# Up products of a half block in two groups by weight part, and w2's pieces loaded in queue order, on one Trainium2 core

## The chip, the cores and the metric

The kernel runs on one core of one Trainium2 chip. The metric is the device time of one execution in microseconds, the median of several runs; lower is better. Before the change it is 1317.91 us (three runs, 1317.73 to 1318.84).

## What is computed

A trunk of two layers over 256 tokens of 1,024 features. Each layer has a feed-forward stage, a mixer and a second feed-forward stage, each followed by a layer norm:

```python
def swiglu(x, w1, w3, w2):
    return (jax.nn.silu(x @ w1) * (x @ w3)) @ w2

for l in range(DEPTH):                       # DEPTH = 2
    x = layer_norm(ALPHA * x + 0.5 * swiglu(x, ffn_w1[l, 0], ffn_w3[l, 0], ffn_w2[l, 0]), ...)
    y, v_raw = hybrid_mixer(x, w_in[l], ..., w_out[l], ...)
    x = layer_norm(ALPHA * x + y, ...)
    x = layer_norm(ALPHA * x + 0.5 * swiglu(x, ffn_w1[l, 1], ffn_w3[l, 1], ffn_w2[l, 1]), ...)
```

w1 and w3 are 1,024 x 2,816, w2 is 2,816 x 1,024, all float32. The mixer (a recurrent branch, a gated branch and a linear recurrence, merged by gates) isn't touched by the change.

## The kernel before

Every large product is made of float32 values split in two: a high part, rounded to the type that TensorE multiplies in one pass, and a low part, the rest. A weight tile is loaded by SP's queue into a raw buffer (`_load`, L73), cast to its high part on ScalarE (L94), and its low part is the difference of the two, on VectorE (L96). The class `Weights` holds all weight tiles of the program in one list in the order of use. It loads some tiles ahead of the conversion and converts four tiles ahead of the use. Tiles of w1 and w3 (four contraction blocks of 128 rows by 256 columns, 512 KB) go through a shared pool of three raw buffers and a ring of five converted pairs. Pieces of w2 (128 rows by 1,024 columns, 512 KB) go through raw buffers of their own, three too, and six converted pairs, both held by the feed-forward stage.

A feed-forward stage takes the 2,816 inner features in 11 blocks of 256. The first block is computed with tokens on the partitions (rows `w1t`, `w3t`). For the other ten, `up(j)` computes features by tokens: for w1 and then for w3, two half blocks of 128 features, each into one PSUM bank (rows `w`). A half block is `feature_wide`: for each of the eight contraction blocks one product of the weights' high part with both parts of the activations, 512 columns (L318), and one of the weights' low part with the activations' high part, 256 columns (L319). The high part's two results lie side by side in the bank, and VectorE adds them (L391). Then comes the gate, and its split into `g`. From the third block on, each `up` is followed by the down products of a block two earlier (rows `dn`, lines L204 to L206 in `mm3`, all 512 columns): 24 products in a row. The last three blocks' down products stand at the end of the stage.

So a stage has ten blocks of four half blocks of 16 products; the four stages of the program have 160 half blocks, 1,280 products of each of the two kinds.

The order in which instructions stand on each engine is made by a planner that knows dependencies, priorities and its own estimate of durations; it moves an instruction ahead of others of its engine when it takes it to be ready. `issue_after` forbids it to put what is issued inside ahead of a given instruction. A load waits for its raw buffer, and SP's queue takes its loads in order.

Of the kernel before, what the change touches and what calls it, by code (L numbers as in the profile page):

```python
# [12 lines left out]
P = 128  # L13
# [39 lines left out]
class Weights:  # L53


    def __init__(self, tc, raw, part, ahead, load_ahead):
        self.nc, self.tc = tc.nc, tc
        self.raw, self.part = raw, part
        self.ahead, self.load_ahead = ahead, load_ahead
        self.queue, self.raws, self.parts = [], {}, {}  # L60
        self.own_raw = None
        self.nload = self.nconv = self.nused = self.hp = 0

    def add(self, key, ap, own=False, pool=False):
# [3 lines left out]
    def _load(self):  # L68
        i = self.nload
        ap = self.queue[i][1]  # L70
        raw = self.own_raw if self.queue[i][2] and self.own_raw else self.raw
        t = raw.tile([P, ap.shape[1], ap.shape[2]], F32, tag="raw", name=f"raw{i}", bufs=3)
        self.last_load = self.nc.sync.dma_start(t, ap).ins  # L73
        self.raws[i] = t
        self.nload += 1

# [42 lines left out]
class Trunk:  # L119
# [193 lines left out]
    def feature_wide(self, out, ws, m):  # L313

        mm = self.nc.tensor.matmul
        for k in range(8):
            hi, lo = (t[:, k % 4, m * P:(m + 1) * P] for t in ws[k // 4])
            mm(out, hi, self.xT2[:, :, k, :], start=k == 0, stop=False)  # L318
            mm(out[:, 0, :], lo, self.xT[0][:, k, :], start=False, stop=k == 7)  # L319

    def queue_block(self, key, w, c0, pool=False):
        for q in range(2):
# [219 lines left out]
class Mixer:  # L542
# [63 lines left out]
    def mm(self, shape, what):  # L606
        return self.T.bank(self.T.mm, shape, what)
# [836 lines left out]
```

## Time and profile before

| what | before |
|---|---|
| median of the runs | 1317.91 us |
| profiled execution | 1319.23 us |
| its span | 1317.5 us |
| TensorE busy | 1289.8 us, 98% of the span |
| VectorE busy | 940.1 us, 71% |
| ScalarE busy | 656.3 us, 50% |
| DMA, mean over the span | 174 GB/s |

The span is the time from the first to the last instruction of the profiled execution; the rest of its 1319.23 us lies around it. An engine is busy while at least one of its instructions is recorded as running. TensorE's products overlap, and the ends in the record are modelled, so the distance between the starts of two products tells what one costs. In the span the feed-forward stages lie at about 8 to 195, 470 to 655, 655 to 842 and 1125 to 1317 us, the mixers between the first and second, and between the third and fourth.

### The profile page before, as it was taken

Reading aid. Unit: us, or ns where it says so; the run is one execution under the profiler, and the core shown is the slowest. Engines: PE = TensorE matmul, PEld = TensorE weight load, DVE = VectorE, ACT = ScalarE, POOL = GpSimd, SP = SyncE. Lnnn points to the kernel's source line nnn. Section 1 sums busy time; section 2 is a strip of 40 time slices with the busy share of each in tenths; the row PEclk is TensorE's granted clock in tenths of the full one; section 3 lists DMA queues with packets and bytes.
Section 4 is the critical chain, followed back from the end, with each engine's and each line's share of the span. In section 5 each row is a group of like instructions: output and inputs, shape, how many; then the busy total and the mean of one; then the engine's idle time right before and its main releaser. Section 6 shows DMA issues by size and latency. Waiting matters only on the chain.

```text
span 1317.5 us, 23323 instructions
## 1 busy us (share of the span) xinstructions
PE 1289.8 (98%) x9527; PEld 1157.5 (88%) x9527; DVE 940.1 (71%) x1311; ACT 656.3 (50%) x881; POOL 84.1 (6%) x147
## 2 busy tenths in 40 slices
PE   9999999998999999999999999999989999999997
PEld 8888889997899988888898888999978998888886
DVE  7786666787676687766686766667867567876664
ACT  6454425655845555444264544275557444544440
POOL 1000000003000110000000000001030002100000
PEclk9999999999999999999999999999989999999999
DMA  9886534534246668665379664264432466776630
GB/s 334 243 265 190 176 96 129 174 114 130 83 129 193 208 228 283 192 189 169 91 271 293 200 187 138 67 185 129 129 98 82 144 210 207 258 246 188 189 111 32
DMA packets 184540, 229.83 MB, mean 174 GB/s; under 512 B 8145, under 2 KB 165841, under 8 KB 184433
## 3 DMA queue, kind: packets, MB, share of 16 engines
q1 hardware_dynamic: 183792, 226.24, 55.5%
q0 software_dynamic: 640, 2.10, 0.5%
q8 instruction: 75, 1.23, 0.4%
q14 instruction: 33, 0.26, 0.1%
HBM read 227.26 MB, written 1.05 MB: 173 GB/s over the span
## 4 chain that ended last, share of the span: by engine, by line
PE 89%; DVE 4%; ACT 3%; POOL 2%; issue 2%; DMA 0%; SPq 0%; DVEq 0%; ACTq 0%; POOLq 0%
PE w L318 23%; PE w L319 11%; PE dn L204 6%; PE dn L205 6%; PE dn L206 6%; PE gate L205 3%; PE gate L204 3%; PE gate L206 3%; PE zr L206 2%; PE zr L205 2%; PE zr L204 2%; PE pb L205 2%; PE pb L206 2%; PE pb L204 2%; DVE wlo L96 1%
## 5 line engine op out<-in xcount | busy, mean ns | idle before, releaser
L94 ACT CAST whi<-raw 128x1024 fp32r<-128x1024 f32 (+1 forms) x322 | 331.7, 1035 | 353.3 <-issue 80.4
L96 DVE TENSOR_TENSOR wlo<-raw,whi 128x1024 fp32r<-128x1024 f32 (+1 forms) x314 | 378.3, 1209 | 166.9 <-ACT whi L94 163.1
L318 PE MATMUL w<-xT,whi 128*128 128x512 f32 x1280 | 452.5, 398 | 0.0
L319 PE MATMUL w<-xT,wlo 128*128 128x256 f32 x1280 | 356.6, 281 | 0.1
L318 PEld LDWEIGHTS w<-xT,whi 128*128 128x128 f32 x1280 | 239.5, 188 | 57.4
L319 PEld LDWEIGHTS w<-xT,wlo 128*128 128x128 f32 x1280 | 241.6, 189 | 3.3 <-DVE wlo L96 0.5
L205 PE MATMUL dn<-w,g 128*128 128x512 f32 x352 | 137.4, 390 | 0.0
L204 PE MATMUL dn<-w,g 128*128 128x512 f32 x352 | 137.1, 391 | 0.0
L206 PE MATMUL dn<-w,g 128*128 128x512 f32 x352 | 137.0, 390 | 0.0
L96 DVE TENSOR_TENSOR w<-raw,w 128x1024 fp32r<-128x1024 f32 x88 | 104.9, 1226 | 37.4 <-ACT w L94 37.4
L391 DVE TENSOR_REDUCE h<-w 128x256 f32<-128x512 f32 x160 | 109.6, 686 | 15.9 <-PE w L319 14.3
L204 PE MATMUL gate<-xT,whi 128*128 128x256 f32 x384 | 110.1, 287 | 1.3 <-DVE xc L1158 1.3
L205 PE MATMUL gate<-xT,whi 128*128 128x256 f32 x384 | 109.7, 286 | 0.0
L206 PE MATMUL gate<-xT,wlo 128*128 128x256 f32 x384 | 109.6, 285 | 0.0
L94 ACT CAST w<-raw 128x1024 fp32r<-128x1024 f32 x88 | 88.7, 1048 | 32.6 <-PE dn L206 23.1
L204 PEld LDWEIGHTS dn<-w,g 128*128 128x128 f32 x352 | 66.1, 188 | 14.6 <-ACT g L209 0.2
L206 PEld LDWEIGHTS dn<-w,g 128*128 128x128 f32 x352 | 66.1, 188 | 14.1
L205 PEld LDWEIGHTS dn<-w,g 128*128 128x128 f32 x352 | 66.1, 188 | 12.2
L204 PEld LDWEIGHTS gate<-xT,whi 128*128 128x128 f32 x384 | 73.4, 191 | 2.5 <-issue 2.2
L205 PEld LDWEIGHTS gate<-xT,whi 128*128 128x128 f32 x384 | 73.4, 191 | 0.8 <-issue 0.2
L206 PEld LDWEIGHTS gate<-xT,wlo 128*128 128x128 f32 x384 | 73.4, 191 | 0.6 <-issue 0.2
L206 PE MATMUL zr<-xT,wlo 128*128 128x256 f32 x224 | 63.9, 285 | 0.0
(333 smaller groups left out, 2205.4 us busy)
## 6 DMA issues: line engine op xcount, KB each, us to landing
raw<-in_ffn_w_dram SPq DMA_DIRECT2D x264, 512.0 KB, 4.6
raw<-in_w_in_dram SPq DMA_DIRECT2D x108, 512.0 KB, 4.1
raw<-in_p_branch_dram SPq DMA_DIRECT2D x24, 512.0 KB, 3.4
raw<-in_w_out_dram SPq DMA_DIRECT2D x16, 512.0 KB, 4.1
ln_g<-in_ln_g_dram SPq DMA_DIRECT2D x8, 256.0 KB, 6.9
ln_b<-in_ln_b_dram SPq DMA_DIRECT2D x8, 256.0 KB, 7.3
bd<-in_bd_dram SPq DMA_DIRECT2D x6, 256.0 KB, 6.0
ln_g<-in_ln_g_dram POOLq DMA_DIRECT2D x4, 256.0 KB, 4.1
```

The costliest lines, as they stand in the source:

```text
L94: self.last_act = self.nc.scalar.copy(hi[:, s:s + w], t[:, s:s + w]).ins
L96: eng.tensor_tensor(lo[:, s:s + w], t[:, s:s + w], hi[:, s:s + w], ALU.subtract)
L204: mm(out, a[0], b[0], start=start, stop=False)
L205: mm(out, a[0], b[1], start=False, stop=False)
L206: mm(out, a[1], b[0], start=False, stop=stop)
L318: mm(out, hi, self.xT2[:, :, k, :], start=k == 0, stop=False)
L319: mm(out[:, 0, :], lo, self.xT[0][:, k, :], start=False, stop=k == 7)
L391: nc.vector.tensor_reduce(t[:, m, :], b.rearrange("p a s -> p s a"), mybir.AxisListType.X, ALU.add)
```

## The change

It has two parts. In `feature_wide` the sixteen products of a half block are written as two loops, the eight of the high part first, then the eight of the low part. A list of the sixteen weight slices is made ahead of them, and the first product still clears the bank and the last closes it. In `_load` a load into a w2 raw buffer may not stand ahead of the last load into a shared raw buffer that was written before it.

```diff
--- before.py
+++ after.py
@@ -58,7 +58,7 @@
         self.raw, self.part = raw, part
         self.ahead, self.load_ahead = ahead, load_ahead
         self.queue, self.raws, self.parts = [], {}, {}
-        self.own_raw = None
+        self.own_raw = self.last_shared = None
         self.nload = self.nconv = self.nused = self.hp = 0
 
     def add(self, key, ap, own=False, pool=False):
@@ -70,7 +70,13 @@
         ap = self.queue[i][1]
         raw = self.own_raw if self.queue[i][2] and self.own_raw else self.raw
         t = raw.tile([P, ap.shape[1], ap.shape[2]], F32, tag="raw", name=f"raw{i}", bufs=3)
-        self.last_load = self.nc.sync.dma_start(t, ap).ins
+        with ExitStack() as order:
+
+            if raw is not self.raw and self.last_shared is not None:
+                order.enter_context(self.tc.issue_after(self.last_shared))
+            self.last_load = self.nc.sync.dma_start(t, ap).ins
+        if raw is self.raw:
+            self.last_shared = self.last_load
         self.raws[i] = t
         self.nload += 1
 
@@ -313,10 +319,11 @@
     def feature_wide(self, out, ws, m):
 
         mm = self.nc.tensor.matmul
+        parts = [[t[:, k % 4, m * P:(m + 1) * P] for k in range(8) for t in ws[k // 4][i:i + 1]] for i in range(2)]
         for k in range(8):
-            hi, lo = (t[:, k % 4, m * P:(m + 1) * P] for t in ws[k // 4])
-            mm(out, hi, self.xT2[:, :, k, :], start=k == 0, stop=False)
-            mm(out[:, 0, :], lo, self.xT[0][:, k, :], start=False, stop=k == 7)
+            mm(out, parts[0][k], self.xT2[:, :, k, :], start=k == 0, stop=False)
+        for k in range(8):
+            mm(out[:, 0, :], parts[1][k], self.xT[0][:, k, :], start=False, stop=k == 7)
 
     def queue_block(self, key, w, c0, pool=False):
         for q in range(2):
```

What this does to the instructions is seen on two engines. TensorE, first stage, right behind the first run of down products: `w_57_656` is the PSUM bank of a half block, `xT_104` the activations, `whi_548` and `whi_554` the high parts of its two weight tiles, `wlo_549` and `wlo_555` the low parts. Before:

```order
L206 MATMUL dn_616<-w_36_505,g_19_378 128x512
L318 MATMUL w_57_656<-xT_104,whi_548 128x512
L319 MATMUL w_57_656<-xT_104,wlo_549 128x256
L318 MATMUL w_57_656<-xT_104,whi_548 128x512
L319 MATMUL w_57_656<-xT_104,wlo_549 128x256
L318 MATMUL w_57_656<-xT_104,whi_548 128x512
L319 MATMUL w_57_656<-xT_104,wlo_549 128x256
L318 MATMUL w_57_656<-xT_104,whi_548 128x512
L319 MATMUL w_57_656<-xT_104,wlo_549 128x256
L318 MATMUL w_57_656<-xT_104,whi_554 128x512
L319 MATMUL w_57_656<-xT_104,wlo_555 128x256
L318 MATMUL w_57_656<-xT_104,whi_554 128x512
```

and now, where a row with x4 is four instructions that read alike:

```order
L212 MATMUL dn_616<-w_36_505,g_19_378 128x512
L324 MATMUL w_57_656<-xT_104,whi_548 128x512 x4
L324 MATMUL w_57_656<-xT_104,whi_554 128x512 x4
L326 MATMUL w_57_656<-xT_104,wlo_549 128x256 x4
L326 MATMUL w_57_656<-xT_104,wlo_555 128x256 x4
L324 MATMUL w_58_674<-xT_104,whi_548 128x512 x4
L324 MATMUL w_58_674<-xT_104,whi_554 128x512 x4
L326 MATMUL w_58_674<-xT_104,wlo_549 128x256 x4
L326 MATMUL w_58_674<-xT_104,wlo_555 128x256 x4
```

The wide products (512) and the narrow ones (256) alternated and now stand in runs of eight; the second half block (`w_58_674`) follows in the same way. Over the whole program there are 160 runs of eight wide and 160 of eight narrow products.

SP's queue at the program's start, behind the loads of the activations and of the first three tiles: tiles of 128x4x256 are w1 and w3, those of 128x1024 are pieces of w2. Before:

```order
L1361 DMA x_94<-in_x_dram 128x1024
L73 DMA raw_381<-in_ffn_w_dram 128x1024
L73 DMA raw_387<-in_ffn_w_dram 128x1024
L73 DMA raw_546<-in_ffn_w_dram 128x1024
L73 DMA raw_142<-in_ffn_w_dram 128x4x256
L73 DMA raw_159<-in_ffn_w_dram 128x4x256
L73 DMA raw_165<-in_ffn_w_dram 128x4x256
L73 DMA raw_552<-in_ffn_w_dram 128x1024
L73 DMA raw_692<-in_ffn_w_dram 128x1024
L73 DMA raw_698<-in_ffn_w_dram 128x1024
L73 DMA raw_227<-in_ffn_w_dram 128x4x256
L73 DMA raw_229<-in_ffn_w_dram 128x4x256
```

and now:

```order
L1368 DMA x_94<-in_x_dram 128x1024
L77 DMA raw_142<-in_ffn_w_dram 128x4x256
L77 DMA raw_159<-in_ffn_w_dram 128x4x256
L77 DMA raw_165<-in_ffn_w_dram 128x4x256
L77 DMA raw_227<-in_ffn_w_dram 128x4x256
L77 DMA raw_229<-in_ffn_w_dram 128x4x256
L77 DMA raw_231<-in_ffn_w_dram 128x4x256
L77 DMA raw_237<-in_ffn_w_dram 128x4x256
L77 DMA raw_243<-in_ffn_w_dram 128x4x256
L77 DMA raw_249<-in_ffn_w_dram 128x4x256
L77 DMA raw_381<-in_ffn_w_dram 128x1024
L77 DMA raw_387<-in_ffn_w_dram 128x1024
```

The pieces of w2 (`raw_381`, `raw_387`, `raw_546` and so on) stood among the first tiles and now follow the tiles that are used ahead of them; their conversions on ScalarE and VectorE moved in the same way. In the later stages the pieces of w2 are put in turn likewise.

## Rows read from the trace of the kernel before

**Rows 1.** The page: TensorE's busy time (share, instructions), granted clock in 40 slices.

```profile
PE 1289.8 (98%) x9527; PEld 1157.5 (88%) x9527; DVE 940.1 (71%) x1311; ACT 656.3 (50%) x881; POOL 84.1 (6%) x147
PEclk9999999999999999999999999999989999999999
```

**Rows 2.** Stretches: us; length; busy us by engine (instructions); clock; DMA share; GB/s.

```profile
330.00:394.00 64.00, 61.37 (x964) 58.13 (x963) 44.47 (x81) 42.84 (x66) 3.26 (x2) 1.00 0.37 109
...
490.00:655.00 165.00, 165.00 (x867) 140.69 (x866) 113.22 (x133) 72.13 (x83) 0.92 (x1) 1.00 0.63 194
...
1140.00:1300.00 160.00, 160.00 (x846) 136.66 (x845) 105.62 (x120) 68.96 (x78) 0.00 (x0) 1.00 0.57 181
```

**Rows 3.** The page's groups: line, engine, names, shapes, count, busy us, mean ns, idle.

```profile
L318 PE MATMUL w<-xT,whi 128*128 128x512 f32 x1280 | 452.5, 398 | 0.0
L319 PE MATMUL w<-xT,wlo 128*128 128x256 f32 x1280 | 356.6, 281 | 0.1
...
L204 PEld LDWEIGHTS gate<-xT,whi 128*128 128x128 f32 x384 | 73.4, 191 | 2.5 <-issue 2.2
```

**Rows 4.** Timeline of TensorE: start us, length us, instruction; down run, up block, down run.

```profile
62.48 0.39 PE L204 MATMUL dn<-w,g 128*128 128x512 f32 x1
...
67.95 0.39 PE L318 MATMUL w<-xT,whi 128*128 128x512 f32 x1
...
79.26 0.39 PE L204 MATMUL dn<-w,g 128*128 128x512 f32 x1
```

**Rows 5.** The same timeline, start of the second feed-forward stage, 17 pairs apart.

```profile
485.11 0.40 PE L318 MATMUL w<-xT,whi 128*128 128x512 f32 x1
...
491.00 0.39 PE L318 MATMUL w<-xT,whi 128*128 128x512 f32 x1
```

**Rows 6.** The same timeline, gate products of layer 0's mixer, 102 products apart.

```profile
406.16 0.28 PE L204 MATMUL gate<-xT,whi 128*128 128x256 f32 x1
...
418.40 0.28 PE L204 MATMUL gate<-xT,whi 128*128 128x256 f32 x1
```

**Rows 7.** Timeline: ninth down product after 62.48; first and 84th of the output projection.

```profile
64.32 0.39 PE L206 MATMUL dn<-w,g 128*128 128x512 f32 x1
...
445.90 0.39 PE L204 MATMUL wo<-whi,mg 128*128 128x512 f32 x1
...
465.12 0.39 PE L206 MATMUL wo<-whi,mg 128*128 128x512 f32 x1
```

**Rows 8.** Timeline: places where up products of one kind already are neighbours.

```profile
31.88 0.88 PE L318 MATMUL w<-xT,whi 128*128 128x512 f32 x3
32.59 0.28 PE L319 MATMUL w<-xT,wlo 128*128 128x256 f32 x1
...
483.00 0.40 PE L318 MATMUL w<-xT,whi 128*128 128x512 f32 x1
...
483.70 0.64 PE L318 MATMUL w<-xT,whi 128*128 128x512 f32 x2
...
484.87 0.40 PE L319 MATMUL w<-xT,wlo 128*128 128x256 f32 x2
```

**Rows 9.** Timeline of VectorE and TensorE at the start, with idle time before and its releaser.

```profile
16.17 2.35 DVE L96 TENSOR_TENSOR w<-raw,w 128x1024 fp32r<-128x1024 f32 x2
18.43 1.22 DVE L96 TENSOR_TENSOR wlo<-raw,whi 128x1024 fp32r<-128x1024 f32 x1
...
18.85 0.40 PE L204 MATMUL w3t<-whi,xT 128*128 128x256 f32 x2
19.71 0.39 PE L205 MATMUL w3t<-wlo,xT 128*128 128x256 f32 x1 [0.46 <-DVE wlo L96]
...
28.42 0.71 PE L318 MATMUL w<-xT,whi 128*128 128x512 f32 x2
...
29.41 0.39 PE L318 MATMUL w<-xT,whi 128*128 128x512 f32 x1
```

**Rows 10.** The page's DMA issues: what, queue, count, KB each, median us to landing.

```profile
raw<-in_ffn_w_dram SPq DMA_DIRECT2D x264, 512.0 KB, 4.6
```

## Prediction

> **What bounds the kernel now.** I began with the page's busy times and its clock line [rows 1]: TensorE holds work in 98% of the span, and its granted clock is at the upper level, 2.4 GHz, in nearly all forty slices. The table of stretches comes next, because the change touches the four feed-forward stages alone [rows 2]: in the two stretches of feed-forward that stand there TensorE has no idle time at all, while the mixer's stretch shown (layer 0, 330 to 394 us) idles 2.6 us. So inside the stages that change, time can only come from how fast TensorE takes its instructions, or from the few waits at the program's start. A busy TensorE is no TensorE at its peak, since a product's recorded length (398 ns for a wide one, 281 for a narrow one, [rows 3]) overlaps the next; I go by distances between starts.
>
> **What an up product costs now.** Between two runs of down products lie 32 pairs, one wide product of the high part (512 columns) and one narrow product of the low part (256). From the first wide start at 67.95 to the first down start at 79.26 is 11.31 us [rows 4], 353.4 ns a pair. There are 1,280 pairs [rows 3], so about 452 us. The pace has a second value: from 485.11 to 491.00 stand 17 pairs, 346.5 ns each [rows 5]. Such stretches cover about 100 pairs, all near the start of stages two to four; 1,180 run at the slower pace. The same two shapes, each among its own kind, give the quicker sum: 102 narrow gate products take 12.24 us, 120.0 ns each [rows 6], and the last 16 of a run of 24 down products, all 512 wide, go from 64.32 to 67.95, 226.9 ns each [rows 4, 7]; 120.0 + 226.9 = 346.9. So alternating costs some 6.5 ns a pair in most places, and a run of one kind seems not to pay it.
>
> **The change part by part.** First, the sequence. No instruction is added or removed: eight wide, then eight narrow products for each of 160 half blocks, 16 instructions each. The printed order shows no half block mixed with another any more; before, a handful near the stages' starts were. Price of eight narrow: 8 x 120.0 = 960 ns [rows 6]; other rows put two neighbours at 118 each (484.87 to 485.11) [rows 5, 8], so 117 to 120 are the ends and I take 120, since the gate products have the same operands. Price of eight wide is the open term, as before never has more than three in a row. Nearest below: 226.9, a settled down run. Nearest above: the three wide ones at 31.88, which reach to 32.59, 237 each [rows 8]. Between them lies the start of a down run, entered from a narrow product as each run of eight will be: its first eight go from 62.48 to 64.32, 230.0 each [rows 4, 7]; and the output projection's 512-wide products never settle, 83 of them at 231.6 [rows 7]. I take 230.0: eight are too few to settle. A half block then takes 8 x 230.0 + 960 = 2,800 ns against 8 x 353.4 = 2,827. For the 1,180 pairs (147.5 half blocks) that is 147.5 x 27 = 4.0 us less; the 12.5 half blocks at 8 x 346.5 = 2,772 lose 12.5 x 28 = 0.35 us. Net -3.6 us. That one pair of equal neighbours already helps is seen at 483.00: six wide and six narrow with one such meeting of each kind take 2.11 us to 485.11, where six pairs at 353.4 take 2.12 [rows 5, 8].
>
> The row on a weight load speaks against a run of narrow products: a load is recorded with 191 ns for a gate product [rows 3]. Were that exclusive, eight narrow would take 1,528 ns and the kernel some 87 us more; but the gates start every 120 ns with a load each [rows 6], so the record overlaps and the load isn't the limit. The Trainium skill ("TensorE: Matmul & The Clock Gate", section "LDWEIGHTS (loading the stationary operand)") gives the columns over 1.2 GHz, an estimate of 107 ns for 128 columns; by that a load fits under a narrow product, with little to spare, and a run of eight costs no more than the gates' 120.
>
> Second, the waits on weights. With the high part first, the low part's subtraction on DVE is needed 8 x 230 = 1.8 us later in a half block; the second tile's high part is needed after 4 x 0.23 = 0.9 us, not after 4 x 0.353 = 1.4. The first tile's low part is held 2.3 us into the second half instead of 1.4, so its buffer comes back 0.9 us later, with a ring of five tiles and two more halves, 5.6 us, before the next block. As no TensorE wait stands in those stretches [rows 2], I cost this at nothing; without that cover it would be at most 0.9 us a block.
>
> Third, w2's pieces asked for in turn. On SP's queue three pieces of w2, needed only by the first down run, stood ahead of the fourth tile of w1/w3, and more after it; now the first pieces stand behind twelve tiles. Their conversions went ahead as well: DVE works on two w2 pieces from 16.17 and only at 18.43 on the low part that TensorE then waits for [rows 9]. Two waits follow: at 18.85 two narrow products take 0.86 us instead of 0.24; at 28.42 two wide and a narrow one take 0.99 instead of 0.57 [rows 9]. Both should go: -1.0 us. Nothing else is late there: the load in question moves up by three places of 512 KB. Later in each stage w2 is queued behind the other loads and its conversions stand in turn on ACT and DVE. SP's queue now stands behind a piece that waits for a free buffer, and the w1/w3 loads with it; but three raw and five converted buffers let them run eight tiles ahead, at four tiles in 16.8 us [rows 4] over 30 us, against 4.6 us to land [rows 10]. Costed at nothing. The planner also shifted some instructions of layer 0's mixer around 320 to 400 us; the stretch idles 2.6 us [rows 2], so I allow 1.5 us either way.
>
> Sum: -3.6 - 1.0 = -4.6 us. The profiled execution took 1319.23 us around a span of 1317.5; the median of the runs is 1317.9. The sum holds against either, and against the median it gives 1313.3.
>
> **The rivals.** (a) Runs of eight settle at once: 8 x 226.9 + 960 = 2,775 ns, 52 less for 147.5 half blocks, -7.7, with the start's -1.0: 1309.2. For it: the good stretch has exactly this pace although the kinds alternate there [rows 5]. Against it: down runs need about five products to get there [rows 7]. (b) The neighbour doesn't matter: a product costs what its width gives, and only the start improves: 1316.9. For it: two narrow in a row at 118, three wide at 237, sum 355, no better than a pair now [rows 8]. The Trainium skill's section "Back-to-back issue gap" on the same page is such a rule, N/2.4 + 2.5 ns, estimates of 216 and 109 ns that the order can't alter; the rows above are 11 ns longer each and show two paces for one mix, so I give it less than the forecast. (c) Slower: the wide product reads two planes of the activations, and a run of such reads on TensorE costs 237 each, as at 31.88: 8 x 237 + 960 = 2,856, 29 more for 147.5 half blocks and 84 more for 12.5, +5.3, less 1.0: 1322.2. It decides from a mean of 233 ns in the run of eight, (2,827 - 960) / 8. Against it: those three fell on a spot just restarted after a wait. (d) w2 in turn comes too late for the down products: each of 36 runs of down products would have to wait, 0.2 us would be enough for +7 less 4.6: 1320.5. The lead of 30 us speaks against it. That the order isn't what the change says is excluded by the printed order.
>
> **How the numbers follow.** Forecast 0.43, (a) 0.23, (b) 0.22, (c) 0.08, (d) 0.04. A change of 0.2%, 2.6 us, is about what a measurement of this kernel can tell from none. Forecast and (a) are faster, 0.66; (b) is within, 0.22; (c) and (d) slower, 0.12. The forecast's own range, with 1.5 us for the mixer, is 1311.8 to 1314.8; the range reaches to (a) and (b), 1308.7 to 1317.6.
>
> **What would show it.** In the trace after, from the first wide start after a down run to the next down start: 11.20 us by the forecast (4 half blocks), 11.10 by (a), 11.31 by (b), 11.42 by (c). Inside a half block the first wide products should stand 230 or more apart and the last near 227. The first up product should start near 21.8 us instead of 22.45, with no wait at 18.9 and 28.4. A new idle time of TensorE in a feed-forward stretch, ended by ACT, DVE or a DMA, would prove the costs at nothing wrong.

## The result: 1.0093 times the time before

The changed kernel takes 1331.08 us (median of four runs, 1329.24 to 1333.86) beside 1317.82 us for the kernel before (four runs, 1317.68 to 1318.84): a ratio of 1.0093, 95% interval 1.0081 to 1.0105, 13.3 us slower. The prediction said 1313.3 us, at most 1317.6. The profiled execution after has a span of 1332.2 us, 14.7 more than the one before.

The page after, to be held against [rows 1] and [rows 3]: TensorE's busy time and clock, the chain that ended last by engine, and the groups of the up products and of ScalarE's casts of w2 (whose tiles are called w; the casts of w1 and w3 write whi):

```profile
PE 1295.6 (97%) x9527; PEld 1163.9 (87%) x9527; DVE 935.0 (70%) x1311; ACT 649.5 (49%) x881; POOL 83.4 (6%) x147
PEclk9999999989999999999999999999989999999999
PE 72%; DVE 9%; DMA 8%; ACT 4%; issue 4%; POOL 2%; SPq 0%; DVEq 0%; ACTq 0%; POOLq 0%
L324 PE MATMUL w<-xT,whi 128*128 128x512 f32 x1280 | 321.4, 393 | 5.7 <-DVE h L398 5.6
L100 ACT CAST w<-raw 128x1024 fp32r<-128x1024 f32 x88 | 92.0, 1050 | 172.1 <-DMA raw<-in_ffn_w_dram 172.1
```

and from the page before, the chain and the casts of w2:

```profile
PE 89%; DVE 4%; ACT 3%; POOL 2%; issue 2%; DMA 0%; SPq 0%; DVEq 0%; ACTq 0%; POOLq 0%
L94 ACT CAST w<-raw 128x1024 fp32r<-128x1024 f32 x88 | 88.7, 1048 | 32.6 <-PE dn L206 23.1
```

TensorE waits 5.6 us for VectorE's reductions (h) ahead of wide up products, where [rows 3] has 0.0. ScalarE waited 172.1 us for w2 to land; before, it idled 32.6 us ahead of these casts, most of it for TensorE. DMA has 8% of the chain that ended last; it was 0% before. One more slice of the clock line shows an 8.

The stretch of [rows 2] from 490 to 655 us, in two pieces (the same columns):

```profile
490.00:630.00 140.00, 140.00 (x754) 121.10 (x753) 88.02 (x101) 59.26 (x67) 0.00 (x0) 1.00 0.64 209
630.00:655.00 25.00, 22.65 (x113) 18.55 (x112) 22.44 (x26) 16.18 (x19) 0.00 (x0) 1.00 0.65 208
```

So the stretch still has no idle time over most of its length, and 2.35 us of it in its last 25 us, towards the stage's end. That is where this stage loses. By the starts of the first and the last down product of each stage, after minus before:

| stretch | before, us | after, us | difference |
|---|---|---|---|
| start to a down run at one place, [rows 4] 62.48 | 62.48 | 60.52 | -2.0 |
| rest of the first feed-forward | 134.5 | 138.0 | +3.5 |
| first mixer | 308.1 | 313.5 | +5.3 |
| second feed-forward | 151.2 | 153.5 | +2.3 |
| between second and third | 35.4 | 35.4 | 0.0 |
| third feed-forward | 151.2 | 154.0 | +2.7 |
| second mixer | 316.1 | 317.8 | +1.8 |
| fourth feed-forward | 150.4 | 151.4 | +1.1 |

They add up to 14.7 us.

**The up block in the middle of a stage** did what the prediction wanted. TensorE's timeline after (start, length, instruction, count), the answer to [rows 4]:

```profile
148.88 0.40 PE L212 MATMUL dn<-w,g 128*128 128x512 f32 x1
149.11 2.00 PE L324 MATMUL w<-xT,whi 128*128 128x512 f32 x8
150.95 1.11 PE L326 MATMUL w<-xT,wlo 128*128 128x256 f32 x8
151.90 2.00 PE L324 MATMUL w<-xT,whi 128*128 128x512 f32 x8
...
160.28 0.39 PE L210 MATMUL dn<-w,g 128*128 128x512 f32 x1
```

Eight wide take 1.84 us (230.0 each), eight narrow 0.95 us (119 each), the block 149.11 to 160.28, 11.17 us against 11.31. From one down run to the next it is 16.63 us, 16.78 before. Inside a run of eight the wide products stand 233, 236, 228, 233 and 231 ns apart and then 227 (medians over the program's runs): as the prediction said, the first ones 230 or more, the last near 227.

**The last two blocks** are another matter. The same timeline right behind, now with idle time before a row and what ended it:

```profile
165.50 0.39 PE L212 MATMUL dn<-w,g 128*128 128x512 f32 x1
166.64 2.08 PE L324 MATMUL w<-xT,whi 128*128 128x512 f32 x8 [0.75 <-DVE h L398]
...
171.36 1.11 PE L326 MATMUL w<-xT,wlo 128*128 128x256 f32 x8
173.52 2.08 PE L324 MATMUL w<-xT,whi 128*128 128x512 f32 x8 [1.05 <-DVE h L398]
...
179.18 0.39 PE L210 MATMUL dn<-w,g 128*128 128x512 f32 x1
...
185.85 0.50 PE L210 MATMUL dn<-w,g 128*128 128x512 f32 x1 [1.06 <-ACT g L215]
```

This cycle takes 18.90 us. From the start of the last down run to its last six products it is 18.08 us, where 15.78 stood before. Who is late shows in the timelines of ScalarE and VectorE over the same time:

```profile
157.31 0.62 ACT L215 CAST g<-gf 128x512 fp32r<-128x512 f32 x1 [1.89 <-DVE gf L381]
163.59 1.05 ACT L100 CAST w<-raw 128x1024 fp32r<-128x1024 f32 x1 [5.66 <-DMA raw<-in_ffn_w_dram]
164.86 1.05 ACT L100 CAST w<-raw 128x1024 fp32r<-128x1024 f32 x1 [0.23 <-DMA raw<-in_ffn_w_dram]
165.82 1.99 ACT L100 CAST whi<-raw 128x1024 fp32r<-128x1024 f32 x2
167.71 1.05 ACT L100 CAST w<-raw 128x1024 fp32r<-128x1024 f32 x1
169.32 1.05 ACT L100 CAST w<-raw 128x1024 fp32r<-128x1024 f32 x1 [0.56 <-DMA raw<-in_ffn_w_dram]
170.28 0.62 ACT L380 ACTIVATE sl<-h 128x512 f32<-128x512 f32 x1
```

```profile
157.96 0.69 DVE L216 TENSOR_TENSOR g<-gf,g 128x512 fp32r<-128x512 f32 x1 [0.69 <-ACT g L215]
164.67 1.23 DVE L102 TENSOR_TENSOR w<-raw,w 128x1024 fp32r<-128x1024 f32 x1 [6.01 <-ACT w L100]
165.81 0.68 DVE L398 TENSOR_REDUCE h<-w 128x256 f32<-128x512 f32 x1
```

Read it backwards. TensorE's wide products at 166.64 need a PSUM bank, which the reduction of 165.81 empties. That reduction stands behind w2's low part on VectorE, which waited 6.01 us for ScalarE's cast, which waited 5.66 us for a piece of w2 to land. Its load and two more were issued behind one of w1/w3, as one row of SP's queue and one of the DMA issues in that window tell:

```profile
156.71 1.86 SPq L77 DMA_DIRECT2D raw<-in_ffn_w_dram  x4
```

```profile
raw<-in_ffn_w_dram SPq DMA_DIRECT2D x4, 512.0 KB, 6.8
```

In turn means behind a load that waits for a raw buffer until 156.71; then four pieces travel together and land 5.6 to 8.0 us later. Four casts of w2 follow close on each other. Between them stand two casts of w1/w3 (165.82), whose tiles had landed at 159.03 and 160.31, and the silu, which is due in between as well, starts only at 170.28.

### The profile page after: what moved, and what is told of

It is laid out like the page before. It is cut to its first block, busy times and chain, and to the rows that moved or that the text cites. A ratio compares the mean times of both kernels' runs of the same rounds, so it can differ in the third digit from the quotient of the medians.

```text
span 1332.2 us, 23244 instructions
## 1 busy us (share of the span) xinstructions
PE 1295.6 (97%) x9527; PEld 1163.9 (87%) x9527; DVE 935.0 (70%) x1311; ACT 649.5 (49%) x881; POOL 83.4 (6%) x147
## 4 chain that ended last, share of the span: by engine, by line
PE 72%; DVE 9%; DMA 8%; ACT 4%; issue 4%; POOL 2%; SPq 0%; DVEq 0%; ACTq 0%; POOLq 0%
PE w L324 16%; PE w L326 8%; DMA raw<-in_ffn_w_dram 7%; PE dn L210 4%; PE dn L212 4%; PE dn L211 4%; DVE wlo L102 4%; PE gate L210 3%; PE gate L211 3%; PE gate L212 3%; PE zr L212 2%; PE zr L211 2%; PE zr L210 2%; PE pb L210 2%; PE pb L212 2%
## 5 line engine op out<-in xcount | busy, mean ns | idle before, releaser
L100 ACT CAST whi<-raw 128x1024 fp32r<-128x1024 f32 (+1 forms) x322 | 328.1, 1032 | 227.3 <-DMA raw<-in_ffn_w_dram 69.1
L324 PE MATMUL w<-xT,whi 128*128 128x512 f32 x1280 | 321.4, 393 | 5.7 <-DVE h L398 5.6
L324 PEld LDWEIGHTS w<-xT,whi 128*128 128x128 f32 x1280 | 231.8, 189 | 51.2 <-issue 5.2
L326 PEld LDWEIGHTS w<-xT,wlo 128*128 128x128 f32 x1280 | 174.6, 190 | 12.6
L326 PE MATMUL w<-xT,wlo 128*128 128x256 f32 x1280 | 178.4, 282 | 0.0
L100 ACT CAST w<-raw 128x1024 fp32r<-128x1024 f32 x88 | 92.0, 1050 | 172.1 <-DMA raw<-in_ffn_w_dram 172.1
L215 ACT CAST g<-gf 128x512 fp32r<-128x512 f32 (+1 forms) x44 | 25.6, 581 | 83.2 <-DVE gf L381 83.2
```

What stands on the lines that cost most here:

```text
L100: self.last_act = self.nc.scalar.copy(hi[:, s:s + w], t[:, s:s + w]).ins
L215: self.split_ins = (self.nc.scalar.copy(hi, src).ins, self.nc.vector.tensor_tensor(lo, src, hi, ALU.subtract).ins)
L324: mm(out, parts[0][k], self.xT2[:, :, k, :], start=k == 0, stop=False)
L326: mm(out[:, 0, :], parts[1][k], self.xT[0][:, k, :], start=False, stop=k == 7)
```

## The experiments

The theories: **A**, w2 in turn makes the loss, through late landings; **B**, the order by parts makes it, since whole runs of high and of low parts are held and asked for. Ratios are to the kernel before, run on the same chip as each (medians of 1319.0 to 1319.2 us).

**The parts alone** (run twice). In the changed kernel's _load:

```diff
-            if raw is not self.raw and self.last_shared is not None:
-                order.enter_context(self.tc.issue_after(self.last_shared))
             self.last_load = self.nc.sync.dma_start(t, ap).ins
```

> Only the first part of the change: up products by parts, w2's pieces issued as the planner likes. Theory A (w2 in turn makes the loss: in the last two blocks of each feed-forward its pieces land late, ScalarE's cast waits, VectorE's reductions and TensorE wait behind it): the cycle from one down run to the next stays at 16.63 us where it was 16.78, the long cycles of 17.75 to 18.93 us at each feed-forward's end go, and the kernel ends 3.5 to 6 us under the kernel before, 1312 to 1314.5 us. Theory B (the order by parts makes the loss, since it asks for all high parts and then all low parts of a half block): the long last cycles stay and the time is 1328 us or more.

> The parts alone once more, beside the run with four ahead on one chip: 1314.5 to 1316.5 us, 0.996 to 0.998 of the kernel before, if the gain of the first part holds.

Measured: 1315.55 us, 0.9968 (0.9955 to 0.9980), and again 1314.61, 0.9963 (0.9949 to 0.9976). The first is 1 us above the range expected, and 3.6 us under the kernel before on that chip, as expected. From the second down run of each stage on, every cycle is 16.63 us to its end, TensorE has no wait in a feed-forward after the first tile, and the chain is as it was. The run from 600 to 665 us, the end of the second feed-forward, of this kernel (second run) and then of the changed one:

```profile
600.00:665.00 65.00, 65.00 (x367) 56.95 (x366) 43.22 (x60) 21.58 (x30) 1.84 (x2) 1.00 0.42 124
```

```profile
600.00:665.00 65.00, 62.62 (x321) 52.51 (x320) 47.18 (x60) 27.87 (x34) 0.92 (x1) 1.00 0.61 194
```

B falls. The first part of the change is a gain of 3.6 and 4.6 us by the medians, 4.2 and 4.9 by the ratios.

**In turn alone**: w2 in turn, up products alternating as before. The list `parts` goes too and is left out here.

```diff
         for k in range(8):
-            mm(out, parts[0][k], self.xT2[:, :, k, :], start=k == 0, stop=False)
-        for k in range(8):
-            mm(out[:, 0, :], parts[1][k], self.xT[0][:, k, :], start=False, stop=k == 7)
+            hi, lo = (t[:, k % 4, m * P:(m + 1) * P] for t in ws[k // 4])
+            mm(out, hi, self.xT2[:, :, k, :], start=k == 0, stop=False)
+            mm(out[:, 0, :], lo, self.xT[0][:, k, :], start=False, stop=k == 7)
```

> Only the second part of the change: w2's pieces asked for in turn, up products alternating as before. Theory A: the cycle is 16.78 us as before, the long last cycles appear (with ScalarE's casts waiting on the weights' DMA and TensorE on VectorE), and the kernel is slower than the changed one by what the order by parts gains, 1333 to 1338 us. Theory B: no long last cycles, 1316 to 1318 us.

Measured: 1332.83 us, 1.0105 (1.0073 to 1.0136). The loss is there without the parts, so A holds for the time. But it is 13.7 us by the medians, hardly more than the changed kernel's 13.3, and just under the range expected: the gain of the parts and the loss don't simply add up. Where it sits was expected only in part: the second feed-forward loses nothing (151.4 us), the first loses 8 us (159.6 where eight cycles of 16.78 give 151.2), in its middle too (cycles of 17.92 and 19.22 us), where TensorE waits for low parts:

```profile
ACT w L100 <- DMA raw<-in_ffn_w_dram: 176.9, 68, 7.3
...
PE dn L210 <- ACT g L215: 2.9, 2, 2.2
...
PE w L325 <- DVE wlo L102: 2.9, 3, 1.6
```

(Who waited for whom: us, times, longest.) The same late stream stops the alternating order at other places.

**How late is too late.** Three kernels leave the parts and let w2 wait for an earlier shared load than the last, n = 1, 2 and 4 loads before its turn. `self.shared` lists the shared loads so far, n stands for the number in each kernel, and the rest of the edit is left out:

```diff
-                order.enter_context(self.tc.issue_after(self.last_shared))
+                order.enter_context(self.tc.issue_after(self.shared[-1 - n]))
```

> The changed kernel, but each piece of w2 waits for the shared load one before its turn (two before: 1319.0, in turn: 1331.1). TensorE's order in the mixers is that of both. If what matters is how many loads that wait for a raw buffer stand ahead of w2, this is the middle dose: 1320 to 1327 us, with last cycles between 16.63 and 18.9 us. If only the last load ahead matters: 1318 to 1320 us, last cycles 16.63.

> The changed kernel, but each piece of w2 waits for the shared load two earlier than its turn, so that it stands two weight loads further ahead in the queue. Theory A: the piece is no longer behind the load that waits for a raw buffer, so the last cycles shrink to 16.6 to 17.0 us and the time to 1310 to 1314 us; if two loads of lead do only half, 1318 to 1325. Theory B: no change from 1331.

> The changed kernel with each piece of w2 waiting for the shared load four before its turn. The feed-forwards are to keep 16.63 us to their ends, as with one and with two ahead (their four stages 150.0, 150.0, 150.0 and 149.1 us long). What is open is the mixers: TensorE's order there is a third one, neither that of the runs with one and two ahead (second mixer 318.2 to 319.2 us from last down run to first, 1317.8 and 1319.0 us in all) nor that of the run with the parts alone (313.7 us, 1315.6 us). If the difference between those runs lies in that order and not in w2, this run lands where its second mixer puts it: 1311 to 1314 us if that takes 313 us, 1317 to 1320 us if it takes 318. If w2 being held at all costs the difference: 1317 to 1319 us with the second mixer at 314 us.

Measured: 1317.84 us, 0.9997 (0.9987 to 1.0007); 1319.00 us, 1.0001 (0.9989 to 1.0013); 1317.73 us, 0.9983 (0.9969 to 0.9997). One load earlier is enough: the four stages, from the first down product to the last, take 150.0, 150.0, 150.0 and 149.1 us in all three, to 0.1 us (before, 151.2 in the second and third and 150.4 in the fourth). I had expected a middle dose from n = 1 and there is none. For n = 2, I had expected 1310 to 1314 us with the waits gone; they are gone, and the time is still 5 us over that range; the second mixer alone takes 4.5 us more than with the parts alone (below). With n = 4 it takes 319.2 us, and the time is what was expected for that case. ScalarE waits for w2 still, but TensorE's waits are gone; the rows of n = 1, then of the changed kernel:

```profile
ACT w L101 <- DMA raw<-in_ffn_w_dram: 97.9, 68, 4.9
```

```profile
ACT w L100 <- DMA raw<-in_ffn_w_dram: 172.1, 64, 6.6
...
PE w L324 <- DVE h L398: 5.6, 6, 1.1
...
PE dn L210 <- ACT g L215: 3.3, 3, 1.2
...
PE dn L212 <- DVE g L216: 0.9, 3, 0.3
```

From the landing of a tile's second w2 piece to its first down product, in the first feed-forward's last three tiles: 56, 45 and 34 us before; 14, 17, 16 in the changed kernel; 23, 23, 25 with n = 1; 29, 29, 32 with n = 2. At these ends the waits are there with leads up to 17 us and gone at 23. The lead alone doesn't decide it: tiles six to eight of the same stage of the changed kernel had 12 to 14 us, and their cycles were 16.63. The n = 1 kernel has TensorE's order of the changed kernel in both mixers (but for small products that overlap, whose recorded starts differ), so the two spans compare directly: 1332.2 - 1316.5 = 15.7 us, of which the four feed-forwards are 14.4 (4.6, 3.5, 4.0 and 2.3 us longer), all of it at their ends.

**The end or the whole stage.** Two kernels split the stage: the last four of eleven tiles free, the others in turn; and only the last three in turn, the others free.

```diff
-            if raw is not self.raw and self.last_shared is not None:
+            if raw is not self.raw and self.last_shared is not None and self.queue[i][0][3] < NFF - 4:
```

```diff
+            if raw is not self.raw and self.last_shared is not None and self.queue[i][0][3] >= NFF - 3:
```

> The changed kernel, but the pieces of w2 for the last four of the eleven tiles of each feed-forward are free of the wait, the others come in turn. Theory A, with the harm decided at the end of a feed-forward alone: the last cycles go back to about 16.63 us and the time to 1311 to 1317 us. If late pieces of the earlier tiles carry the delay to the end as well: 1322 to 1331 us. Theory B: 1331 us.

> Up products by parts; of w2 only the pieces of the last three of the eleven tiles of each feed-forward are asked for in turn, all others as the planner likes. The program's TensorE order outside the feed-forward products is that of the run with the parts alone. Theory A with the harm in the six pieces that stand in a row at a feed-forward's end: the cycles there are 17.7 to 18.9 us again, each feed-forward gives 2 to 4 us, and the time is 1323 to 1330 us. If lateness has to build up over the earlier tiles: cycles of 16.63 us to the end and 1314 to 1317 us.

Measured: 1318.88 us, 1.0001 (0.9987 to 1.0015), and 1314.62 us, 0.9971 (0.9959 to 0.9983). Neither has the long cycles at the end. The first lies between the two ranges expected for it. It has four cycles of 17.0 to 17.4 us, none of them among the last two blocks, and its feed-forwards take 2.2 us more than those of n = 1. In the second it was not the first of the two outcomes, which I held likelier, but the other. So neither the row of six pieces at the end, nor a late stream over the first tiles, is enough alone for the loss at the ends. With the last three in turn alone their lead is 22 to 24 us, not 14 to 17, so that kernel doesn't try late pieces of w2 at the end by themselves. The up weights go with it: they land 20 us ahead of their use there and before, and 8 to 13 us ahead in the late tiles of the changed kernel. That alone does no harm at the end either, since they are as late in the kernel with the free tail. In turn from the first tile, the whole stream runs later: a cast of w2 that waits on ScalarE holds back the casts of w1/w3 behind it, these free their raw buffers later, SP's next load of w1/w3 waits for one, and w2 stands behind that. The two casts at 165.82 above are one turn of it. This loop is read from the rows; what was tried is that either part of the stage in turn costs the feed-forwards at most 2.2 us.

**The carrier.** w2's cast and low part on GpSimd, all in turn:

```diff
-            self.last_act = self.nc.scalar.copy(hi[:, s:s + w], t[:, s:s + w]).ins
-            eng = self.nc.gpsimd if pool else self.nc.vector
+            if own and self.own_raw is not None:
+                self.nc.gpsimd.tensor_copy(hi[:, s:s + w], t[:, s:s + w])
+            else:
+                self.last_act = self.nc.scalar.copy(hi[:, s:s + w], t[:, s:s + w]).ins
+            eng = self.nc.gpsimd if pool or own and self.own_raw is not None else self.nc.vector
```

> The changed kernel with w2 in turn, but w2's cast and low part are made by GpSimd instead of ScalarE and VectorE. If the late pieces reach TensorE through the queues of ScalarE and VectorE (silu and the reductions stand behind the casts that wait), TensorE's waits on VectorE at each feed-forward's end go though w2 lands as late as before, and the time is 1316 to 1322 us. If the down products need w2 itself sooner than it lands, TensorE waits for GpSimd there and the time stays at 1328 us or more; a GpSimd subtraction took 2,409 ns where VectorE takes 1,230, which may add to it.

Measured: 1340.24 us, 1.0170 (1.0151 to 1.0190). The time is that of the second outcome, the waits are those of the first. The cycle of 18.90 us is 16.63, and TensorE's waits on VectorE and ScalarE in the feed-forwards, but for one row at three stages' ends, go from 9.8 us to 0.3, as they should if the queues of ScalarE and VectorE carried them. The up weights of the late tiles land 16 to 20 us ahead again, as they should if w2's casts on ScalarE had held theirs back. But GpSimd needs 2,973 ns for a subtraction, VectorE's own of w1/w3 take 1,543 ns on average beside it instead of 1,230, and the planner ordered the last down products differently: those that VectorE's layer norm needs first are done 14.3 us into the last run, 9.3 before. The transposes of its result stand ahead of the last six down products, as before, and TensorE waited for them in three stages:

```profile
191.67 0.39 PE L215 MATMUL dn<-w,g 128*128 128x512 f32 x1
196.14 1.97 PE L289 MATMUL tr<-ident,x 128*128 128x128 f32 x8 [4.08 <-DVE x L258]
197.76 0.78 PE L213 MATMUL dn<-w,g 128*128 128x512 f32 x1
```

The program's end, behind the last down product, is 5.3 us longer as well. The kernel speaks for the carrier, but its own order changed too, so it proves nothing by itself; its time says nothing about w2 in turn. A kernel that moves nothing but the place of w2's casts on ScalarE was not run.

**In turn where it helps**: the parts, and w2 in turn among the first 42 loads alone.

```diff
-            if raw is not self.raw and self.last_shared is not None:
+            if raw is not self.raw and self.last_shared is not None and i < 42:
```

> Up products by parts; w2 in turn only among the first 42 loads, that is for the first six or so tiles of the first feed-forward. Theory A: the startup is that of the changed kernel (the down run that began at 62.48 us before and at 61.93 with the parts alone begins at 60.5), the feed-forwards keep 16.63 us to the end, and the time is 1 to 1.5 us under the parts alone, 1313 to 1315 us, give or take 3 us for the mixers, which the planner orders a little differently.

Measured: 1318.57 us, 1.0001 (0.9991 to 1.0010): no gain, and just above the range expected, with its 3 us for the mixers. The feed-forwards are right (150.0, 150.0, 149.1), but the mixers took 314.9 and 317.9 us, with w2 free around the second.

**The mixers.** TensorE's order in the mixers differs between these kernels, though no edit touches them; the planner orders the whole program anew. The second mixer took 313.6 to 313.7 us in the three profiles with one order (the parts alone, twice, and the tail in turn), 316.1 before, and 317.8 to 319.2 in the changed kernel and in n = 1, 2, 4, the free tail and the start in turn. These have other orders, and in the last of them w2 is free there. The kernel with w2 on GpSimd has still another order, all of w2 in turn, and 314.4 us. So it is the order and not w2's wait that makes most of it. With a granted clock of 0.99 in this mixer in each, the order is worth some 4 us (313.6 against 317.8); the 319.2 of n = 1 and n = 4 go with 0.98. This is why no version with w2 held back at the start came out better than the parts alone, which is the fastest version found, 0.9963 and 0.9968; the tail in turn equals it.

In the first mixer the changed kernel loses 3.1 us to n = 1 with the same order and no idle time. Seven us of each, at the same place in the program (columns as in [rows 2]):

```profile
269.00:276.00 7.00, 7.00 (x32) 6.43 (x32) 2.08 (x6) 0.58 (x1) 1.64 (x1) 0.52 0.04 13
```

```profile
265.00:272.00 7.00, 7.00 (x58) 6.69 (x57) 3.44 (x7) 1.76 (x4) 1.64 (x1) 1.00 0.03 9
```

The granted clock stands at 0.52, so at the lower level of 1.2 GHz nearly all the time, and 32 products pass where 58 do at 2.4 GHz. TensorE had no idle time in the 19 us ahead of it. That late w2 brought it on is not shown: the tail in turn, without a wait at its stages' ends, has such a stretch there as well:

```profile
264.00:274.00 10.00, 10.00 (x45) 9.31 (x46) 3.85 (x9) 1.68 (x3) 1.64 (x1) 0.52 0.07 23
```

and the same place ran at 1.00 in the parts alone, with the same order. Over the whole first mixer the granted clock is 0.97 in three profiles, where it takes 313.4 us (the changed kernel), 315.3 (the tail in turn) and 314.9 (the start in turn), and 0.99 in the parts alone and n = 1, 2 and 4, where it takes 310.3 to 310.9. Each kernel has one profile, and the granted clock differs between executions of one kernel (0.989 to 0.994 over the twelve of the second run of the parts alone; the changed kernel's profile is the lowest of its four, 0.989 against 0.992 to 0.994, and its span is 2.5 to 4.7 us longer than theirs). So these 3.1 us may belong to the execution and not to the change. Their cause stays open. Another 2.2 to 2.8 us of the first mixer's +5.3 are in the parts alone too (310.3 and 310.9 us); the half-clock stretch that follows 4 us of idle time of TensorE there lasted 6.8 us in them and 3.4 in the profile of before.

## Why the prediction was wrong

**What bounds the kernel, and the up products: right.** Taken at 230.0 and 120.0 ns, they came at 230.0 and 119; the block is 11.17 us, between the forecast's 11.20 and rival (a)'s 11.10. A stage without other trouble takes 150.0 us instead of 151.2 from its first down product to its last, eight cycles of 0.15 us less. Four stages give -4.9 us against the predicted -3.6, mostly because the narrow products came 1 ns quicker than taken. The wide ones settle in the sixth of eight, later than (a) had it. The two blocks ahead of the first down run gain nothing: 35.4 us between the second and third stages, as before. With the parts alone the kernel took 0.9963 to 0.9968 of its time before, -4.2 to -4.9 us. Rival (b) is refuted by the 16.78 that became 16.63. The Trainium skill's "Back-to-back issue gap" ("TensorE: Matmul & The Clock Gate") gives N/2.4 + 2.5 ns as the gap of an isolated product and has no term for the order; its 216 and 109 ns (estimates) are not reached here by runs of one kind, at 230.0 and 119. Rival (c), eight wide products at 237 ns each, did not come either. The three at 31.88 on which it rested stood 2.7 us behind the end of the wait at 28.42, not just behind it as the prediction had it; 233 and 236 ns are what the first two products of a run of eight take here, and the last three take 227.

**The start: right in kind.** TensorE's rows at the place of [rows 9] hold no wait now:

```profile
20.98 0.28 PE L212 MATMUL w3t<-whi,xT 128*128 128x256 f32 x1
21.10 2.00 PE L324 MATMUL w<-xT,whi 128*128 128x512 f32 x8
```

The first up product starts at 21.10 us (said: 21.8; before: 22.45), and the down run of [rows 4] begins 1.96 us earlier. Counted from the first tile's first product (7.63 us, 8.05 before), the first up product comes 0.9 us earlier. Not all of that is the change's: TensorE's wait of 0.4 to 0.5 us for a low part, between 18 and 20 us, stands in each profile in which the start is as before (the parts alone, twice, and the tail in turn) and in none with the start in turn; but the first tile's first product began anywhere from 7.1 to 8.5 us in these profiles, so the exact share can't be told from them.

**w2 in turn "costed at nothing": this step failed**, and with it the range. It rested on a lead of over 30 us, worked out from eight tiles of buffers at the pace of [rows 4], against 4.6 us to land [rows 10]. Three things were wrong in that. Buffers bound how far loads may run ahead, they don't tell how far they do: the up weights led by 20 us before, and w2's lead of up to 56 us at the stage's end came from its free place in the queue, the very thing that the change took away. The landing time is a median over all; behind a queue that had waited, four pieces took 5.6 to 8.0 us. And I looked for the harm at the down products (rival (d), 0.2 us for each of 36 runs), whose w2 is still 14 us early; it came through ScalarE and VectorE, where an early-placed cast of w2 holds the silu and the reductions behind it. The prediction named that queueing ("its conversions stand in turn on ACT and DVE") and put no price on it. Measured, against n = 1: 2.3 to 4.6 us at each of four stage ends, 14.4 in all.

**"A new idle time in a feed-forward stretch ended by ACT, DVE or a DMA"** was given as the sign that would prove it wrong, and is what the trace shows: 9.8 us in 12 waits.

**The mixers: the term was too small.** ±1.5 us stood for them; they gave +5.3 and +1.8 here and -2.4 in the second mixer of the parts alone. Of the +5.3, most goes with the granted clock of that profile, which the prediction could not know. Against the prediction's sum: -4.6 became -6.8 from the start and the parts (2.0 to the down run of [rows 4], 1.1 in the rest of the first stage, 1.2 in each other), +14.4 at the stages' ends and +7.1 in the mixers: 14.7 us.

## What to carry to other kernels

When a transfer is moved back in an in-order queue, count its lead in the trace, landing to the instruction that first waits for it; here that is its conversion, not the product that uses it, and whatever stands behind the conversion on that engine waits along. A change with two halves is run as two kernels: here one half gains about 4 us, and the other costs three times as much. Where a planner orders the program, a change in one stage reorders others far away, and that moved a mixer by some 4 us.

## What was not expected of the hardware

A first run of eight wide products after a wait takes 1.93 us (166.64 to 168.57) instead of 1.84. And the row of a wait counts from the recorded end of the product before, by when the next would long have started: the cycle of 18.90 us is 2.27 longer, and its two rows show 1.80, so each such wait cost some 0.24 us beyond its row. For 12 rows that is some 3 of the 4.6 us by which the loss of 14.4 exceeds their 9.8. Four transfers of 512 KB issued within 1.9 us landed 1.3 us apart, the last 8.0 us after its issue, where the median of all is 4.9. And the granted clock fell to the lower level for 6.8 and 10.2 us in a mixer where TensorE showed no idle time, in some profiles and not in others with the same order.
